# Low halves and sums of the feed-forward part shared between VectorE and GpSimd, and inputs laid out by the host, in a hybrid decoder layer

## The chip, the cores and the metric

One core of one Trainium2 chip runs the whole layer. The metric is the device time of one execution in microseconds (us). The engines are TensorE (PE; its weight loads are PEld in the profile), VectorE (DVE), ScalarE (ACT), GpSimd (POOL) and SyncE (SP), which issues every DMA of this kernel.

## What is computed

The layer takes 2048 tokens of width 1024 in float32. It has a combined projection, a short causal convolution beside dilated attention, an output projection, a feed-forward part with a gated convolution, and a gate on a per-layer input `p`:

```python
h = rmsnorm(x, g_mix[i]);  z = h @ w_in[i]
zb, zc, zx, zq, zk, zv = jnp.split(z, ...)
y_c = zb * causal_dwconv3(zc * zx, conv_w[i], conv_b[i])
y_a = dilated_attention(rmsnorm(zq), rmsnorm(zk), zv)      # three dilations, merged
x = x + concatenate([rmsnorm(y_c, g_out_conv[i]), rmsnorm(y_a, g_out_attn[i])]) @ w_out[i]
h = rmsnorm(x, g_ffn[i])
gate = causal_dwconv3(h @ w_gate[i], ffn_conv_w[i], ffn_conv_b[i])
x = x + (jax.nn.silu(gate) * (h @ w_up[i])) @ w_down[i]    # D_FF = 2816
x = x + sigmoid(rmsnorm(x, g_ple[i]) @ w_ple_gate[i]) * (p[i] @ w_ple_proj[i])
```

## The kernel before

**Precision by halves.** Each operand of a product is split in two. `split` lets ACT copy the float32 value to the reduced type (the high half, L91) and another engine subtract that from the value (the low half, L92). `mm3` (L95) then makes three matmuls: high by high, high by low, low by high. A product on 128x512 tiles is a run of such triples in one PSUM bank.

**Stages.** `qkv` makes q, k and v (until about 347 us of the profile). `mix` runs attention with the convolution's matmuls woven between (until about 995 us). `rest` holds what follows: `project` (the output projection; part 0 of the token groups 0 and 1 first, from 995 us, then part 1, then both parts of groups 2 and 3), `prepare` (normalised tokens as the right-hand operands of the feed-forward part), `gate_up` and `down`, each run for two halves `h` of the tokens, `prepare_ple` and `ple`.

**The feed-forward part** saves matmuls by combining blocks before and after (seven products where eight would stand). `gate_up` runs over `f` = 0 to 10, once per half. For each `f` it makes seven products of gate and seven of up (168 matmuls of 128x512). `left` makes the seven weight operands from raw tiles: four sums on DVE (L706) and seven splits, low halves on POOL. DVE reads the products from PSUM (L757, L991, L1000, L1002), applies the two tap lines of the convolution (L257, L258) and multiplies (L1003); POOL makes four sums of the results (`combined`, L1011). In the first half two side jobs run along: `sums_of_w_down` loads two tiles of `w_down`, makes four differences on POOL (L963) and stores them, for each `f`; `for_later` normalises the other half's tokens on DVE (L792) and stores them. `down` splits one activation tile (low half on DVE) and one weight tile (low half on POOL) for every twelve matmuls, adds earlier sums on POOL (L1052), and meanwhile lets `right` prepare the next stage's operands: differences on DVE (L726), and low halves on the engine that each `put` names.

**What sets the order.** The instructions of an engine run in the order in which a scheduler put them down when the kernel was built. It works from its own estimate of times, so a change in one place can shift the order elsewhere. An engine that waits for one operand holds back all that stands behind it. SP issues DMAs in one such row too.

**Loads of tokens.** The tokens of `x`, `p` and the output are used in an order in which 32 neighbouring rows of a tile lie 16 rows apart in memory. `tokens` (L69) therefore issues four DMAs per tile, one for each group of 32 partitions. `qkv` loads 16 tiles of `x` this way, `project` 32 half tiles, `ple` 16 tiles of `p` and 32 half tiles of output. The convolution's taps `fcw`, `fcb`, `cw`, `cb` and the gains `go`, `gk`, `gq` are read one element at a time.

```python
def split(self, hi, lo, src, lo_engine):
    self.nc.scalar.copy(hi, src)
    lo_engine.tensor_tensor(lo, src, hi.bitcast(F32), ALU.subtract)
```

## Time and profile before

| | us |
|---|---|
| median of 3 runs (2838.21 to 2851.06) | 2841.0 |
| the profiled execution | 2845.52 |
| its span | 2843.8 |
| PE busy in the span | 2638.9 (93%) |
| DVE busy | 1908.9 (67%) |
| POOL busy | 1520.2 (53%) |
| ACT busy | 1320.3 (46%) |

The profile is of one execution. Matmuls are pipelined and their ends are modelled, so the share of a busy PE says less than where PE stood idle and what ended that. The list of waits names, for each engine and line, what it waited for. A timeline gives single instructions with their duration; a table of windows gives busy times in stretches that are named by their start and end in us from the span's start, with the granted clock of PE (1.00 is 2.4 GHz, 0.50 is 1.2 GHz), the DMA engines' busy share and the rate.

### The profile page before, as it was taken

Reading aid. Unit: us, or ns where it says so; the run is one execution under the profiler, and the core shown is the slowest. Engines: PE = TensorE matmul, PEld = TensorE weight load, DVE = VectorE, ACT = ScalarE, POOL = GpSimd, SP = SyncE. Lnnn points to the kernel's source line nnn. Section 1 sums busy time; section 2 is a strip of 40 time slices with the busy share of each in tenths; the row PEclk is TensorE's granted clock in tenths of the full one; section 3 lists DMA queues with packets and bytes.
Section 4 is the critical chain, followed back from the end, with each engine's and each line's share of the span. In section 5 each row is a group of like instructions: output and inputs, shape, how many; then the busy total and the mean of one; then the engine's idle time right before and its main releaser. Section 6 shows DMA issues by size and latency. Waiting matters only on the chain. (4 is left out here: it accounts for less than half of the span.)

```text
span 2843.8 us, 38213 instructions
## 1 busy us (share of the span) xinstructions
PE 2638.9 (93%) x12320; PEld 2174.1 (76%) x12320; DVE 1908.9 (67%) x3355; ACT 1320.3 (46%) x2941; POOL 1520.2 (53%) x1050
## 2 busy tenths in 40 slices
PE   6999989999899869899889999999999999998998
PEld 5777778888788658677677787877878777786787
DVE  8776656767676555987767778457677776647543
ACT  3322257767768234453334444444444445444332
POOL 4111311624343724478786678575666668767554
PEclk9999989999899989999999999999999999999999
DMA  6444566675755778665552236673323326665343
GB/s 185 149 136 124 174 151 152 182 173 148 196 154 152 213 222 306 195 224 205 199 193 97 97 125 213 232 240 106 101 102 104 112 89 212 222 227 195 97 124 88
DMA packets 374473, 470.10 MB, mean 165 GB/s; under 512 B 51072, under 2 KB 214528, under 8 KB 374272
## 3 DMA queue, kind: packets, MB, share of 16 engines
q1 hardware_dynamic: 374272, 467.66, 53.2%
q8 instruction: 97, 1.59, 0.2%
q14 instruction: 104, 0.85, 0.1%
HBM read 339.53 MB, written 127.99 MB: 164 GB/s over the span
## 5 line engine op out<-in xcount | busy, mean ns | idle before, releaser
L95 PE MATMUL ps<-t,w 128*128 128x512 f32 x4368 | 1034.4, 396 | 45.9 <-DVE u L757 23.1
L95 PEld LDWEIGHTS ps<-t,w 128*128 128x128 f32 x4368 | 819.8, 189 | 247.2 <-DVE u L757 28.7
L92 POOL TENSOR_TENSOR w<-raw,w 128x512 fp32r<-128x512 f32 x318 | 477.3, 1510 | 298.4 <-ACT w L91 281.9
L92 POOL TENSOR_TENSOR w<-s,w 128x512 fp32r<-128x512 f32 x208 | 298.8, 1441 | 178.4 <-ACT w L91 172.4
L95 PE MATMUL ps<-w,g 128*128 128x512 f32 x1368 | 342.6, 399 | 52.9 <-ACT g L828 22.3
L95 PEld LDWEIGHTS ps<-w,g 128*128 128x128 f32 x1368 | 258.2, 191 | 118.8 <-ACT g L828 24.9
L290 POOL TENSOR_TENSOR clo<-craw,chi 128x512 fp32r<-128x512 f32 x96 | 125.8, 1317 | 394.7 <-ACT chi L289 132.1
L95 PE MATMUL zps<-hq,chi 128*128 128x512 f32 x768 | 257.1, 412 | 9.2 <-DVE yc L329 5.9
L91 ACT CAST w<-raw 128x512 fp32r<-128x512 f32 x318 | 192.5, 615 | 94.1 <-PE ps L95 90.8
L91 ACT CAST w<-s 128x512 fp32r<-128x512 f32 x208 | 127.9, 617 | 228.3 <-PE ps L95 196.2
L95 PE MATMUL ps<-w,t 128*128 128x512 f32 x852 | 212.1, 395 | 6.8 <-POOL w L92 4.7
L440 ACT ACTIVATE pt<-so,md 128x256 f32<-128x256 f32 (+1 forms) x384 | 174.9, 457 | 84.5 <-DVE md L437 82.6
L95 PEld LDWEIGHTS ps<-w,t 128*128 128x128 f32 x852 | 160.8, 190 | 44.8 <-POOL w L92 7.3
L437 DVE CUSTOM_DVE_ANT_0 so<-s,neg 128x256 f32<-128x256 f32 (+1 forms) x384 | 130.3, 362 | 64.8 <-PE s L434 53.1
L706 DVE TENSOR_TENSOR s<-raw 128x512 f32<-128x512 f32 x88 | 113.4, 1289 | 83.4 <-POOL w L92 82.5
L95 PEld LDWEIGHTS zps<-hq,chi 128*128 128x128 f32 x768 | 142.1, 196 | 35.2 <-DVE yc L329 7.2
L92 DVE TENSOR_TENSOR g<-g 128x512 fp32r<-128x512 f32 x84 | 97.2, 1162 | 98.2 <-ACT g L91 93.2
L95 PE MATMUL zps<-hq,clo 128*128 128x512 f32 x384 | 154.5, 403 | 0.0
L433 PE MATMUL s<-kk,qs 128*128 128x256 f32 (+1 forms) x384 | 132.9, 353 | 20.6 <-DMA kk<-kd 18.2
L434 PE MATMUL s<-kk,qs 128*128 128x256 f32 (+1 forms) x384 | 137.1, 361 | 14.8 <-DMA v<-vd 5.8
L174 POOL TENSOR_TENSOR raw<-hT 128x1024 f32<-128x1024 f32 x16 | 39.0, 2438 | 202.4 <-DVE rs_h L78 187.5
L473 DVE TENSOR_TENSOR nb<-po,nb 64x512 f32<-64x512 f32 x96 | 92.1, 959 | 63.9 <-ACT nb L472 62.9
(214 smaller groups left out, 5118.4 us busy)
## 6 DMA issues: line engine op xcount, KB each, us to landing
gd<-t SPq DMA_DIRECT2D x110, 256.0 KB, 2.0
craw<-in_w_in_dram SPq DMA_DIRECT2D x96, 256.0 KB, 4.0
raw<-in_w_gate_dram SPq DMA_DIRECT2D x44, 512.0 KB, 3.7
raw<-in_w_up_dram SPq DMA_DIRECT2D x44, 512.0 KB, 3.5
g<-gd SPq DMA_DIRECT2D x84, 256.0 KB, 4.3
raw<-td SPq DMA_DIRECT2D x40, 512.0 KB, 4.0
t<-gd SPq DMA_DIRECT2D x70, 256.0 KB, 4.3
v<-vd SPq DMA_DIRECT2D x264, 64.0 KB, 2.6
```

The costliest lines, as they stand in the source:

```text
L91: self.nc.scalar.copy(hi, src)
L92: lo_engine.tensor_tensor(lo, src, hi.bitcast(F32), ALU.subtract)
L95: mm = lambda *a, **k: self.nc.tensor.matmul(*a, **k, **kw)
L174: nc.gpsimd.tensor_tensor(t, hT[:, :, 0].bitcast(F32), hT[:, :, 1].bitcast(F32), ALU.add)
L290: nc.gpsimd.tensor_tensor(lo, raw, hi.bitcast(F32), ALU.subtract)
L433: mm(s[:, lo:], qb[l], cols[0], start=True, stop=False)
L434: mm(s[:, lo:], qb[l], cols[1], start=False, stop=True)
L437: nc.vector.tensor_tensor_reduce(out=so[:, lo:], in0=s[:, lo:], in1=neg[:, br, lo:], scale=-slope, scalar=3.0e38, op0=ALU.add, op1=ALU.min ...
L440: nc.scalar.activation(pt[:, l, lo:], so[:, lo:], AF.Exp, bias=md[:, 0, col:col + 1], scale=-1.0, accum_out=md[:, 1, col:col + 1])
L473: nc.vector.tensor_tensor(dst, like(po[other], br), dst, ALU.add)
L706: nc.vector.tensor_tensor(t, x, y, op)
```

## The change

Three things are changed.

- **Two of three low halves and sums go to VectorE.** A new method `shared` counts calls and returns DVE twice, then POOL once. It now names the engine for the low halves of all weight operands of `project`, `gate_up` and `down`, of the left operands of `ple`, for the sums of squares before `project` and for the sums L1052 in `down`.
- **Fixed moves to VectorE.** The four differences of `sums_of_w_down` go to DVE, as do two of the four sums in `combined` (the other two stay on POOL), two of the four fixed `put`s in `right`, and all low halves that `prepare_ple` names by its own engine.
- **Layout by the host.** `lay_out` permutes `x`, `p` and the weights before the launch, and the output is permuted back after it. `tokens` becomes one DMA per tile. The weight tiles of `w_in`, `w_gate` and `w_up` and the small vectors are contiguous for each partition.

```diff
     def tokens(self, tile, dram, c, j, store=False):
-        for b in range(4):
-            rows, part = dram[c, 4 * j + b], tile[32 * b:32 * b + 32]
-            self.nc.sync.dma_start(*((rows, part) if store else (part, rows)))
+        self.nc.sync.dma_start(*((dram[c, j], tile) if store else (tile, dram[c, j])))
...
+    def shared(self):
+        self.turn = (self.turn + 1) % 3
+        return self.nc.vector if self.turn else self.nc.gpsimd
...
-                nc.sync.dma_start(gk[64 * i:64 * i + 64], a["k_norm_g"].rearrange("(d o) -> d o", o=1))
...
+                nc.sync.dma_start(gk, a["k_norm_g"])
...
-                    nc.sync.dma_start(raw, wv[:, k:k + 2, c0:c0 + 512])
+                    nc.sync.dma_start(raw, a["w_qkv"][w, :, k:k + 2])
...
-            nc.sync.dma_start(raw, self.a["w_in"].rearrange("(k p) n -> p k n", p=P)[:, k:k + 4, c0:c0 + P])
+            nc.sync.dma_start(raw, self.a["w_conv"][z, :, k:k + 4])
...
-                        yield w.rearrange("(k p) n -> p k n", p=P)[:, :, 2 * f * P:2 * f * P + 2 * P]
+                        yield w[f]
...
-                        self.split(t[:, 0], t[:, 1], raw[0][:, i], nc.gpsimd)
+                        self.split(t[:, 0], t[:, 1], raw[0][:, i], self.shared())
...
-            for i in range(3):
-                nc.sync.dma_start(cw[:, :, i], a["ffn_conv_w"][i].rearrange("(k p) -> p k", p=P))
-            nc.sync.dma_start(cb, a["ffn_conv_b"].rearrange("(k p) -> p k", p=P))
+            nc.sync.dma_start(cw, a["ffn_conv_w"])
+            nc.sync.dma_start(cb, a["ffn_conv_b"])
...
-                    self.split(view(t[:, 0]), view(t[:, 1]), x, nc.gpsimd)
+                    self.split(view(t[:, 0]), view(t[:, 1]), x, self.shared())
...
-                put(4, t1, nc.gpsimd)
+                put(4, t1, nc.vector)
...
-                put(6, t3, nc.gpsimd)
+                put(6, t3, nc.vector)
...
-                    nc.gpsimd.tensor_tensor(ssq, ssq, y, ALU.add)
+                    self.shared().tensor_tensor(ssq, ssq, y, ALU.add)
...
-                minus = lambda t, x, y: nc.gpsimd.tensor_tensor(t, x, y, ALU.subtract)
+                minus = lambda t, x, y: nc.vector.tensor_tensor(t, x, y, ALU.subtract)
...
-                        nc.gpsimd.tensor_tensor(t, x, y, op)
+                        (nc.gpsimd if m in (3, 6) else nc.vector).tensor_tensor(t, x, y, op)
...
-                            nc.gpsimd.tensor_tensor(x, x, addend[j], ALU.add)
+                            self.shared().tensor_tensor(x, x, addend[j], ALU.add)
...
-                                     [b[0], b[3], b[1], b[2]], nc.gpsimd)
+                                     [b[0], b[3], b[1], b[2]], nc.vector)
...
+def lay_out(a):
+    by = lambda t, shape, *axes: np.ascontiguousarray(t.reshape(shape).transpose(axes))
+    tokens = lambda t: by(t, (NQ, 32, 16, -1), 0, 2, 1, 3).reshape(SEQ, -1)
...
+        w_gate=by(a["w_gate"], (KD, P, NF // 2, 2 * P), 2, 1, 0, 3), w_up=by(a["w_up"], (KD, P, NF // 2, 2 * P), 2, 1, 0, 3),
```

The lines behind each changed place shift by a few numbers: L69 becomes L66, L92 becomes L94, L706 becomes L702, L757 becomes L753, L963 becomes L959.

SP in the first part of `project`. The names are: `t` rows of x to be added to, `e` and `s` rows of the attention's and the convolution's results (`yad`, `ycd`), `xd` the stored sums. Before:

```order
L823 DMA e<-yad_85 128x512
L823 DMA e<-yad_86 128x512
L823 DMA e<-yad_87 128x512
L823 DMA e<-yad_88 128x512
L69 DMA t<-in_x_dram 32x512 x2
L908 DMA xd_93<-t 128x512
L908 DMA xd_94<-t 128x512
L69 DMA t<-in_x_dram 32x512
L908 DMA xd_95<-t 128x512
L908 DMA xd_96<-t 128x512
L69 DMA t<-in_x_dram 32x512 x13
L823 DMA s<-ycd_81 128x512
```

And with the change:

```order
L328 DMA ycd_84<-yc 128x512
L66 DMA t<-in_x_dram 128x512 x8
L819 DMA e<-yad_85 128x512
L819 DMA e<-yad_86 128x512
L819 DMA e<-yad_87 128x512
L819 DMA e<-yad_88 128x512
L819 DMA s<-ycd_81 128x512
L819 DMA s<-ycd_82 128x512
L819 DMA s<-ycd_83 128x512
```

The loads `s<-ycd` stood behind a long run of issues for x and behind the stores `xd` of token group 1; they now follow eight whole loads of x and four of `e`, ahead of any store.

DVE in `gate_up` of the first half, within one `f` (f = 2): `u`, `e` and `t` are results from PSUM and rows made of them, `s` sums of raw weight tiles, `w` weight operands, `g` tiles of `w_down`. Before:

```order
L757 TENSOR_TENSOR u_14076<-ps_13996,u_14015 128x512
L991 TENSOR_TENSOR e_14097<-ps_13997,u_14076 128x512
L251 MEMSET e_14118 128x2
L706 TENSOR_TENSOR s_14284<-raw_14078,raw_14079 128x512
L991 TENSOR_TENSOR e_14118<-ps_13996,u_14015 128x512
L706 TENSOR_TENSOR s_14286<-s_14284,raw_14078 128x512
L257 SCALAR_TENSOR_TENSOR t_14120<-e_14118,fcw_11136,t_14120 128x512
L991 TENSOR_TENSOR e_14151<-ps_13997,u_14032 128x512
```

And with the change:

```order
L753 TENSOR_TENSOR u_13925<-ps_13845,u_13864 128x512
L257 SCALAR_TENSOR_TENSOR t_13900<-e_13898,fcw_11083,t_13900 128x512
L987 TENSOR_TENSOR e_13946<-ps_13846,u_13925 128x512
L250 MEMSET e_13967 128x2
L959 TENSOR_TENSOR g_15378<-g_15379,g_15378 128x512
L702 TENSOR_TENSOR s_14133<-raw_13927,raw_13928 128x512
L94 TENSOR_TENSOR w_13985<-raw_13774,w_13985 128x512
L959 TENSOR_TENSOR g_15379<-g_15379,g_15378 128x512
L959 TENSOR_TENSOR g_15379<-g_15379 128x512
L987 TENSOR_TENSOR e_13967<-ps_13845,u_13864 128x512
L94 TENSOR_TENSOR w_14041<-s_14039,w_14041 128x512
L702 TENSOR_TENSOR s_14135<-s_14133,raw_13927 128x512
```

Low halves (L94) and differences of `w_down` (L959) now stand between the reads from PSUM.

POOL in `down` of the first half, where every low half of a weight tile stood:

```order
L92 TENSOR_TENSOR w_17726<-raw_17683,w_17726 128x512
L92 TENSOR_TENSOR w_17759<-raw_17683,w_17759 128x512
L92 TENSOR_TENSOR w_17781<-raw_17724,w_17781 128x512
L92 TENSOR_TENSOR w_17803<-raw_17724,w_17803 128x512
L92 TENSOR_TENSOR w_17825<-raw_17779,w_17825 128x512
L92 TENSOR_TENSOR w_17844<-raw_17779,w_17844 128x512
```

And with the change:

```order
L94 TENSOR_TENSOR w_17381<-raw_17316,w_17381 128x512
L94 TENSOR_TENSOR w_17444<-raw_17379,w_17444 128x512
L94 TENSOR_TENSOR w_17510<-raw_17467,w_17510 128x512
L94 TENSOR_TENSOR w_17575<-raw_17532,w_17575 128x512
L94 TENSOR_TENSOR w_17652<-raw_17573,w_17652 128x512
```

Of two tiles of one raw load both stood on POOL; now every third tile of the stream does, and the others stand on DVE.

## Rows read from the trace of the kernel before

**Rows 1.** The page, busy time, share of the span and instructions of each engine.

```profile
PE 2638.9 (93%) x12320; PEld 2174.1 (76%) x12320; DVE 1908.9 (67%) x3355; ACT 1320.3 (46%) x2941; POOL 1520.2 (53%) x1050
```

**Rows 2.** Waits of PE, 0 to 50 us: us in total, times, longest.

```profile
PE ps L95 <- DVE hT L125: 4.7, 1, 4.7
PE tp L122 <- DVE rs_h L78: 4.0, 1, 4.0
```

**Rows 3.** Waits of PE, 995 to 1066 us (first part of `project`).

```profile
PE ps L95 <- ACT g L828: 22.3, 3, 18.2
```

**Rows 4.** Waits of PE, 1235 to 1470 us (`gate_up`, first half, f 0 to 4).

```profile
PE ps L95 <- DVE u L757: 17.7, 11, 4.1
PE ps L95 <- ACT w L91: 5.8, 2, 5.1
PE ps L95 <- POOL w L92: 3.8, 4, 1.4
```

**Rows 5.** Waits of PE, 1450 to 2660 us.

```profile
PE ps L95 <- POOL w L92: 31.9, 31, 3.8
PE ps L95 <- DVE u L757: 6.2, 4, 2.5
```

**Rows 6.** Windows: us, PE, PEld, DVE, ACT, POOL busy (instructions), PEclk, DMA share, GB/s.

```profile
995.00:1000.00 5.00, 3.20 (x14) 2.31 (x14) 3.58 (x6) 1.38 (x3) 0.00 (x0) 1.00 0.89 6
...
995.00:1066.00 71.00, 46.76 (x198) 36.84 (x198) 36.06 (x66) 25.79 (x42) 19.46 (x14) 0.86 0.77 220
1066.00:1140.00 74.00, 74.00 (x339) 60.76 (x338) 41.79 (x90) 31.43 (x66) 30.95 (x23) 1.00 0.85 301
...
1140.00:1235.00 95.00, 84.47 (x381) 66.78 (x380) 85.31 (x135) 51.52 (x101) 43.31 (x30) 0.96 0.60 198
...
1272.50:1466.10 193.60, 169.97 (x724) 134.06 (x723) 137.10 (x137) 74.59 (x159) 158.67 (x107) 0.96 0.60 209
1466.10:1700.50 234.40, 231.02 (x996) 186.38 (x995) 171.79 (x192) 98.37 (x211) 154.64 (x107) 1.00 0.33 110
```

**Rows 7.** Timeline of DVE, 1356 to 1362 us: start, duration, instruction.

```profile
1356.76 1.77 DVE L706 TENSOR_TENSOR s<-raw 128x512 f32<-128x512 f32 x1
...
1361.79 0.68 DVE L757 TENSOR_TENSOR u<-ps,u 128x512 f32<-128x512 f32 x1
```

**Rows 8.** Timeline of POOL, the same stretch.

```profile
1356.24 1.73 POOL L92 TENSOR_TENSOR w<-raw,w 128x512 fp32r<-128x512 f32 x1
```

**Rows 9.** Single lines, whole run: duration in ns, min/median/max, first and last start.

```profile
L706 DVE TENSOR_TENSOR s<-raw x88: 675/1760/1787, 1208.8 to 2341.9; 128x512 f32<-128x512 f32 x88
...
L757 DVE TENSOR_TENSOR u<-ps,u x104: 673/678/694, 1244.9 to 2826.0; 128x512 f32<-128x512 f32 x104
...
L258 DVE SCALAR_TENSOR_TENSOR t<-e,fcw,t x88: 735/1549/1783, 1251.2 to 2365.4; 128x512 f32<-128x512 f32 x88
...
L92 POOL TENSOR_TENSOR w<-raw,w x318: 1267/1304/2348, 937.8 to 2599.9; 128x512 fp32r<-128x512 f32 x159
```

**Rows 10.** Groups by line, 1272.5 to 1466.1 us: busy, mean ns, idle before.

```profile
L706 DVE TENSOR_TENSOR s<-raw 128x512 f32<-128x512 f32 x16 | 25.1, 1567 | 22.8 <-POOL w L92 22.8
...
L963 POOL TENSOR_TENSOR g<-g 128x512 f32<-128x512 f32 x34 | 50.1, 1475 | 24.7 <-DMA g<-in_w_down_dram 19.2 <-issue 2.7 <-DVE u L1002 2.4
```

**Rows 11.** Timeline of SP, 992 to 1037 us: start, time to issue, DMAs.

```profile
992.67 3.94 SPq L682 DMA_DIRECT2D fcw<-in_ffn_conv_w_dram  x3
...
1003.55 11.34 SPq L69 DMA_DIRECT2D t<-in_x_dram  x18
...
1030.08 5.90 SPq L69 DMA_DIRECT2D t<-in_x_dram  x13
1036.08 0.37 SPq L823 DMA_DIRECT2D s<-ycd  x1
```

**Rows 12.** Timeline of SP at the start.

```profile
4.53 2.27 SPq L69 DMA_DIRECT2D xt<-in_x_dram  x4
```

**Rows 13.** Timeline at the end, last stores of the output.

```profile
2836.87 4.50 SPq L69 DMA_DIRECT2D out_dram<-s  x8
```

More of the change, by code (lines that the diff above doesn't have):

```diff
@@ L45, in __init__ @@
         nc = self.nc
+        self.turn = 0
         self.const = ctx.enter_context(tc.tile_pool(reuse_waits="tile", name="const", bufs=1))
@@ L60, in __init__ @@
         self.td = [d.tile([NF // 2, P, 2, 512], F32, name=f"td{i}") for i in range(2)]
-        self.xq = a["x"].rearrange("(c a b) m -> c b a m", a=32, b=16)
-        self.pq = a["p"].rearrange("(c a b) m -> c b a m", a=32, b=16)
-        self.oq = out.rearrange("(c a b) m -> c b a m", a=32, b=16)
+        self.xq, self.pq, self.oq = [t.rearrange("(c j r) m -> c j r m", c=NQ, r=P) for t in (a["x"], a["p"], out)]
     def tokens(self, tile, dram, c, j, store=False):
-        for b in range(4):
-            rows, part = dram[c, 4 * j + b], tile[32 * b:32 * b + 32]
-            self.nc.sync.dma_start(*((rows, part) if store else (part, rows)))
+        self.nc.sync.dma_start(*((dram[c, j], tile) if store else (tile, dram[c, j])))
     def rsqrt(self, pool, ss, n, scale):
@@ L145, in gains @@
             def gains():
-                for i in range(2):
-                    nc.sync.dma_start(gk[64 * i:64 * i + 64], a["k_norm_g"].rearrange("(d o) -> d o", o=1))
-                    nc.sync.dma_start(gq0[64 * i:64 * i + 64], a["q_norm_g"].rearrange("(d o) -> d o", o=1))
+                nc.sync.dma_start(gk, a["k_norm_g"])
+                nc.sync.dma_start(gq0, a["q_norm_g"])
                 for p in range(4):
@@ L154, in qkv @@
             whl = {w: [(wvp if w == 2 else wp).tile([P, KD, 512], F32R, name=f"w{w}{s}") for s in "hl"] for w in range(3)}
-            wv = a["w_in"].rearrange("(k p) n -> p k n", p=P)
             def load_w(w):
@@ L159, in load_w @@
                     raw = stage.tile([P, 2, 512], F32, name="raw", tag="raw")
-                    c0 = 3 * CW + 512 * w
-                    nc.sync.dma_start(raw, wv[:, k:k + 2, c0:c0 + 512])
+                    nc.sync.dma_start(raw, a["w_qkv"][w, :, k:k + 2])
                     self.split(whl[w][0][:, k:k + 2], whl[w][1][:, k:k + 2], raw, nc.gpsimd if w or k % 4 else nc.vector)
@@ L281, in load_conv_w @@
         nc, pool = self.nc, self.cwp
-        c0 = CW * (1, 2, 0)[n % 3] + P * (n // 3 % 4)
+        z = 4 * (1, 2, 0)[n % 3] + n // 3 % 4
         halves = []
@@ L300, in conv @@
         cb = cp.tile([P, 4], F32, name="cb")
-        for i in range(3):
-            nc.sync.dma_start(cw[:, :, i], a["conv_w"][i].rearrange("(k p) -> p k", p=P))
-        nc.sync.dma_start(cb, a["conv_b"].rearrange("(k p) -> p k", p=P))
+        nc.sync.dma_start(cw, a["conv_w"])
+        nc.sync.dma_start(cb, a["conv_b"])
         carry = cp.tile([P, 4, 2, 2, 1], F32, name="carry")
@@ L676, in rest @@
             go = cp.tile([P, 2, 4], F32, name="go")
-            for i, n in enumerate(("g_out_conv", "g_out_attn")):
-                nc.sync.dma_start(go[:, i], a[n].rearrange("(k p) -> p k", p=P))
+            nc.sync.dma_start(go, a["g_out"])
             cw = cp.tile([P, NF, 3], F32, name="fcw")
             cb = cp.tile([P, NF], F32, name="fcb")
-            for i in range(3):
-                nc.sync.dma_start(cw[:, :, i], a["ffn_conv_w"][i].rearrange("(k p) -> p k", p=P))
-            nc.sync.dma_start(cb, a["ffn_conv_b"].rearrange("(k p) -> p k", p=P))
+            nc.sync.dma_start(cw, a["ffn_conv_w"])
+            nc.sync.dma_start(cb, a["ffn_conv_b"])
             carry = cp.tile([P, NF, 2, 1], F32, name="fcarry")
@@ L1183, in steps @@
     return r
+def lay_out(a):
+    by = lambda t, shape, *axes: np.ascontiguousarray(t.reshape(shape).transpose(axes))
+    tokens = lambda t: by(t, (NQ, 32, 16, -1), 0, 2, 1, 3).reshape(SEQ, -1)
+    w_in, g_out = a.pop("w_in"), np.stack([a.pop("g_out_conv"), a.pop("g_out_attn")])
+    return dict(
+        a, x=tokens(a["x"]), p=tokens(a["p"]), g_out=by(g_out, (2, 4, P), 2, 0, 1),
+        w_conv=by(w_in[:, :3 * CW], (KD, P, 12, P), 2, 1, 0, 3), w_qkv=by(w_in[:, 3 * CW:], (KD, P, 3, 512), 2, 1, 0, 3),
+        conv_w=by(a["conv_w"], (3, 4, P), 2, 1, 0), conv_b=by(a["conv_b"], (4, P), 1, 0),
+        q_norm_g=np.tile(a["q_norm_g"], 2)[:, None], k_norm_g=np.tile(a["k_norm_g"], 2)[:, None],
+        w_gate=by(a["w_gate"], (KD, P, NF // 2, 2 * P), 2, 1, 0, 3), w_up=by(a["w_up"], (KD, P, NF // 2, 2 * P), 2, 1, 0, 3),
+        ffn_conv_w=by(a["ffn_conv_w"], (3, NF, P), 2, 1, 0), ffn_conv_b=by(a["ffn_conv_b"], (NF, P), 1, 0))
 def build(shapes):
@@ L1203 @@
     arrays = {n: np.ascontiguousarray(v[0]) for n, v in arrays.items()}
+    arrays = lay_out(arrays)
     arrays["steps"] = steps()
@@ L1206 @@
     r = run_bass_kernel_spmd(nc, [{f"in_{n}_dram": v for n, v in arrays.items()}], core_ids=[0])
-    return r.results[0]["out_0_dram"].reshape(1, SEQ, D)
+    return np.asarray(r.results[0]["out_0_dram"]).reshape(NQ, 16, 32, D).transpose(0, 2, 1, 3).reshape(1, SEQ, D)
```

## The prediction

> **What bounds the kernel now.** I read the busy line first [rows 1]: PE is busy 93% of the span of 2843.8 us, DVE 67%, POOL 53%. PE executes the same matmuls after the change, so what can be won is the time in which PE stands idle, 2843.8 − 2638.9 = 205 us. Busy shares can't tell which of it this change reaches; the waits of PE by stage can, so I read those next. In the stages that the change touches they are: 8.7 us at the start [rows 2], 22.3 in the first part of `project`, one of them 18.2 long [rows 3], 27.3 in f0 to f4 of `gate_up` [rows 4], and 31.9 on low halves from POOL in all that follows, 31 waits of about 1 us [rows 5]. `mix` keeps its order of matmuls and its engines; I give it nothing. The windows [rows 6] say what a stage takes when nothing is late: six `f` of the first half take 234.4 us with PE busy for 231.0, so 39.1 us each; the four before them take 193.6, so 37 are lost there.
>
> Timelines of DVE and POOL in that stretch show why DVE's `u` comes late there. L706, a sum of two tiles in SBUF, takes 1.77 us while a low half runs on POOL beside it [rows 7, 8]; L757, which reads PSUM, takes 0.68 next to it. Over the whole run L706 takes 0.675 at least and 1.76 at the median, L757 never more than 0.69, and POOL's low half 1.30 at the median and 2.35 at most [rows 9]. So a POOL instruction that meets a two-input one of DVE costs DVE up to 1.76 − 0.68 = 1.08 us. Taking POOL instructions away therefore shortens DVE's other work, and this is what pays for most of the work that DVE gets.
>
> **The change part by part.** *The start.* A whole tile of x is one issue and not four of 2.27 us together [rows 12], and the gains come in fewer DMAs. PE's two waits there end on the norm of these tokens [rows 2]. I take 4 of 8.7; ends 0 and +8.
>
> *First part of `project`.* SP needs 3.94 us for three loads of taps, 11.34 for 18 quarter tiles of x and 5.90 for 13 more; only at 1036.08 does it come to `s<-ycd`, on which L828 waits, and PE with it [rows 11, 3]. By the new order eight whole loads of x stand there and `s<-ycd` ahead of any store. 31 issues in 17.2 us are 0.56 each, so 24 quarters fewer are 13 us of issuing. At the stretch's beginning the DMA engines are 0.89 busy at 6 GB/s [rows 6], with the taps read element by element; that also goes. How much can be won? The stage moves 220 GB/s × 71 us = 15.6 MB, which at the 301 GB/s of the next stretch [rows 6] takes 52 us; so 19 at most. I take 16; ends 8 and 20. The transfers may be the next thing that is late.
>
> *`prepare` of the first half and `project` of groups 2 and 3* (1140 to 1235 us): DVE is already busy for 85.3 of 95 us [rows 6]. It gets about two thirds of the low halves of this stretch, some 20 × 0.68 = 13 us. Against that stand up to 20 meetings with POOL less, at 1.08 each. I take 0; ends −6 and +6.
>
> *`gate_up`, f1 to f4 of the first half.* DVE and POOL run in lockstep here: DVE's L706 waits 22.8 us for POOL's low halves, and POOL, with 158.7 of 193.6 us busy, waits another 19.2 at L963 for `w_down` [rows 6, 10]. In f1 to f3 the new order gives DVE 174 instructions where it had 102: 36 differences L959, 28 low halves, 6 sums and 2 others. At their shortest durations [rows 9] (33 reads of PSUM at 0.68, 26 of the tap lines at 0.74, the rest at 0.68) that is about 120 us against 70, or 40 per `f`. POOL keeps 14/3 = 4.67 low halves and 2 sums per `f`, which cost DVE 6.67 × 1.08 = 7.2 us if each meets one of its instructions. So DVE needs 47 us per `f`, and becomes the bound for three `f`; the fourth may run at 39.1. 3 × 47 + 39.1 = 180 against 193.6: a gain of 13.5. But POOL's waits for `w_down` in these three `f`, some 19.2 × 3/4 = 14, may now be DVE's, with the reads of PSUM behind them: then 194. PE is late by whichever DVE does last. I take +4; ends −10 (both the waits and half of the former loss) and +14. If nothing met on the two engines, the term would be 193.6 − 4 × 40 = +34; that is the first rival.
> The Trainium skill ("SBUF — State Buffer", section "SBUF: two separate sides") states that the pair of ports which VectorE and GpSimd share is an exclusive lock held for a whole instruction, and that the loser blocks fully. In that form a meeting costs DVE the whole POOL instruction, which the row has at 1.30 us and not 1.08: over the 20 POOL instructions of f1 to f3 that is 4.4 us more and would take this term to about 0, the forecast to about 2803. The durations of L706 (1.76 at the median, 1.79 at most, against 0.68 alone) bear out the blocking but put its price at 1.08.
>
> *Low halves after 1450 us.* 31.9 us of waits have POOL's low half as their last releaser [rows 5]: in-order POOL at 1.3 us per tile, with sums and stores of other stages between. Two thirds of the low halves leave POOL, so 21 us of these waits go with them. The third that stays finds a less crowded POOL: I let half of 10.6 go, +5. DVE's own new waits (low halves behind reads of PSUM, or the other way round: `u` waits were 6.2 here [rows 5]) I put at −8, somewhat more than these 6.2. Sum +18; ends +5 and +28.
>
> *Steady `gate_up`* (the rest of the first half, the second half; 17 `f`): DVE has 192 instructions in six `f`, 171.8 us busy [rows 6]; 32 per `f`, 21.3 us at their shortest, the other 7.3 us being stretch. It gets 9.33 low halves and 2 sums: 29.0. With 6.67 POOL instructions at 1.08 it is 36.2 of 39.1 us. So it fits with 7% to spare: 0, and this is the tightest place of the whole sum. The other end is 1 to 1.2 us for each of the 17 where in-order waits use up the spare, −20; +5 at best, since PE's 3.4 idle us in six `f` leave no more.
>
> *The end.* The last stores take 4.50 us of issuing for eight [rows 13]; two whole ones instead: +1.5, ends 0 and +3.
>
> Sum: 4 + 16 + 0 + 4 + 18 + 0 + 1.5 = 43.5 us. Against the profiled execution, 2845.5 (span and 1.7 around it), this is 2802. That execution lies 4.5 us above the median of the runs, 2841.0, so the forecast is 2841.0 − 43.5 = 2797.5.
>
> **The rivals.** *Better: the two engines no longer meet.* If POOL's few instructions fall into DVE's idle times or beside reads of PSUM, DVE needs 40 us per `f` in f1 to f3, all of rows 4 and nearly all of rows 5 goes, and the terms become 8, 19, 6, 34, 28, 5, 3: 103 at the very most. A half of the step from 43.5 to there gives 2768, and I let this case span 2740 to 2770. For it: POOL is busy for less than half of what it was. Against: today's median of L706 is the stretched one [rows 9], and six or seven POOL instructions per `f` stay. Chance 0.18.
>
> *Slower: DVE takes POOL's place as the bound.* DVE is in-order, and each low half must wait for ACT's high half, with reads of PSUM queued behind it, for which PE's banks wait. With 36.2 of 39.1 us used, it decides when DVE loses over 7% of its time to such waits. At 15% an `f` takes 36.2/0.85 = 42.6, which is 3.5 more, times 17: −60; f1 to f3 take 47/0.85 = 55 each, so that term is 193.6 − 204 = −10; of the low-half waits 5 are left as gain, and start, `project` and end keep their 21.5. Net −44: 2885; at 12%, 41.1 and 53.4 each, the terms are −35, −6, +5 and +21.5, so −14 and 2855. For it: 30 to 37 of DVE's instructions per `f` then stand in one row with the PSUM reads. Against: at 1140 to 1235 us DVE is busy for 90% [rows 6] with PE still busy for 89%. Chance 0.10, with 2850 to 2885.
> The exclusive lock of the Trainium skill's page "SBUF — State Buffer" (same section) would speak for this rival, since with 1.30 a meeting DVE's 36.2 would be 37.7 of 39.1.
>
> *The loads of `project` are hidden behind another limit.* If not SP's issuing but the transfers or the stores of `yad` and `ycd` end last, the wait [rows 3] shrinks by 5 and not 16. For it: the DMA engines are 0.77 busy in this stretch. Against: `s<-ycd` itself is only issued at 1036 [rows 11]. 2797.5 + 11 = 2808.5; together with the lower half of the low-half term it reaches 2815 to 2835. Chance of this case 0.17: two thirds of it end near 2820 to 2835, within 0.5% of before or close to it.
>
> *That the change does not do what it says* I can exclude: in its instruction order the low halves stand on DVE, and the loads of x are whole.
>
> **How the numbers follow.** Forecast 0.55, within 2778 to 2815. Better 0.18, the loads and small gains 0.17, slower 0.10. The range leaves out the far half of the better case and the slower case: 2756 to 2838. About 0.5% of 2841, 14 us, is what a measurement of this kernel can tell from no change: faster means below 2827, slower above 2855. Faster: the forecast, the better case and a third to a half of the third, 0.77; same 0.15; slower 0.08, the part of the slower case above 2855.
>
> **What would show each step.** In the profile after: SP's issues of x whole, `s<-ycd` issued before about 1025 us, and the 18.2 us wait on L828 gone; if it only moves to a DMA, the third case holds. DVE's L702 with a median below the 1.76 of L706. DVE busy at 2000 to 2100 us, POOL at 700 to 800. In f1 to f4 a spacing near 47 us, in the others 39 to 39.5; 41 or more there is the slower case, 40 or 41 in f1 to f3 the better one. PE's waits on POOL's low halves after 1450 us down to 5 to 10 us; waits on DVE's `u` or DVE's low halves above 15 us would say that DVE took over what POOL gave up. What would make the prediction wrong most easily is this last point: work moved to the engine that drains PSUM.

## The result, and the profile after

| | us | ratio to before, 95% interval |
|---|---|---|
| before, median of 4 | 2842.9 | |
| changed, median of 4 (2758.95 to 2762.15) | 2760.3 | 0.9707 [0.9683, 0.9731] |
| changed, profiled execution | 2758.95 | |

The change takes 82.5 us off the median, nearly twice the 43.5 that the forecast names; the time lies in its range, near the low end. The two profiled executions differ by 86.6. The table puts that difference to stages: it compares when PE starts the n-th of its 12320 matmuls in each profile, counted in time order. (A few matmuls change places in the feed-forward part, so a border there is good to a microsecond or so. From the last start to the end of the span it is 7.0 us before and 6.3 after, which the table leaves out.) The last two columns are for two experiments described below, the layout alone (E1) and the moves alone (E2).

| matmuls | stage | before | changed | gain | E1 | E2 |
|---|---|---|---|---|---|---|
| first start | | 10.9 | 9.0 | 1.9 | 8.7 | 11.2 |
| 0 to 1400 | `qkv` | 322.8 | 320.3 | 2.5 | 319.1 | 320.9 |
| 1400 to 4800 | `mix`, mainly | 666.2 | 651.4 | 14.8 | 655.9 | 658.9 |
| 4800 to 5000 | `project`, first part | 69.7 | 51.8 | 17.9 | 50.2 | 67.9 |
| 5000 to 5900 | `project`, `prepare`, f0 and f1's start | 216.1 | 207.4 | 8.7 | 215.6 | 210.6 |
| 5900 to 6600 | `gate_up` f1 to f4, mainly | 188.0 | 172.1 | 15.9 | 186.8 | 169.7 |
| 6600 to 7650 | f5 to f10 | 246.9 | 242.1 | 4.8 | 246.7 | 242.1 |
| 7650 to 9000 | `prepare`, `down` | 329.9 | 326.1 | 3.8 | 330.8 | 326.4 |
| 9000 to 10300 | `gate_up`, second half | 308.2 | 300.3 | 7.9 | 308.2 | 300.3 |
| 10300 to the last start | `down`, `ple` | 477.9 | 470.4 | 7.5 | 476.5 | 470.4 |

The busy line of the page after, to be held against [rows 1]: DVE has 523 instructions more and only 98 us more to do, POOL half of its instructions and half of its time. PE's busy time is 17.4 us less for the same 12320 matmuls, with a mean granted clock of 0.983 where it was 0.977. So a fifth of the 86.6 us does not come out of idle time, as far as the modelled ends of matmuls tell.

```profile
PE 2621.5 (95%) x12320; PEld 2169.0 (79%) x12320; DVE 2006.8 (73%) x3878; ACT 1321.2 (48%) x2941; POOL 784.3 (28%) x527
```

**First part of `project`.** SP's issues, as in [rows 11], and PE's waits from 975 to 1035 us, as in [rows 3]. The taps are one issue, and x comes in whole tiles. Four loads `s<-ycd` go out ahead of x, at 975, as they did before; the one that [rows 11] have at 1036.08, behind the loads of x, is now issued at 987.67. That is 7 us after PE starts the stage, and it was 36. The wait on ACT's `g` is 1.1 us where it was 22.3, and the stage moves 310 GB/s (window below; columns as in [rows 6]).

```profile
972.17 0.44 SPq L678 DMA_DIRECT2D fcw<-in_ffn_conv_w_dram  x1
...
975.22 2.31 SPq L819 DMA_DIRECT2D s<-ycd  x4
...
979.81 3.84 SPq L66 DMA_DIRECT2D t<-in_x_dram  x8
...
987.67 2.44 SPq L819 DMA_DIRECT2D s<-ycd  x3
```

```profile
980.70:1033.00 52.30, 46.91 (x203) 37.53 (x202) 37.17 (x73) 26.26 (x43) 8.69 (x6) 0.97 0.93 310
```

```profile
PE ps L97 <- DVE t L902: 3.2, 1, 3.2
PE ps L97 <- DVE yc L327: 3.1, 1, 3.1
PE ps L97 <- ACT g L824: 1.1, 1, 1.1
```

**f1 to f4 of the first half.** The windows are the single `f`, cut where PE starts each one's first product; columns as in [rows 6]. After the change f1, f2 and f3 take 46.5, 44.9 and 45.9 us, f4 38.9 and the ones behind it 193.9 / 5 = 38.8. In f1 to f3 DVE is busy for 124.3 of 137.3 us, POOL for 36.5.

```profile
1234.00:1280.50 46.50, 43.01 (x200) 34.56 (x198) 42.69 (x59) 21.05 (x44) 15.17 (x7) 1.00 0.82 280
1280.50:1325.40 44.90, 41.90 (x189) 33.36 (x188) 39.20 (x57) 18.50 (x40) 11.92 (x7) 1.00 0.85 279
1325.40:1371.30 45.90, 41.86 (x169) 33.53 (x168) 42.45 (x62) 17.45 (x37) 9.40 (x6) 0.93 0.74 262
1371.30:1410.20 38.90, 38.90 (x170) 31.58 (x170) 30.45 (x44) 16.76 (x36) 10.78 (x7) 1.00 0.31 108
1410.20:1604.10 193.90, 193.90 (x841) 157.75 (x840) 154.81 (x220) 83.30 (x176) 51.09 (x33) 1.00 0.31 104
```

Cut in the same way, four later `f` of the kernel before give 159.2 / 4 = 39.8 each:

```profile
1511.40:1670.60 159.20, 156.23 (x673) 125.90 (x672) 118.19 (x130) 65.88 (x141) 103.95 (x72) 1.00 0.30 101
```

PE's waits from 1180 to 1415 us (against [rows 4]) and from 1400 to 2570 us (the cut of [rows 5]), and DVE's own waits in f1 to f3:

```profile
PE ps L97 <- DVE w L94: 9.0, 5, 4.0
PE ps L97 <- POOL w L94: 2.2, 1, 2.2
PE ps L97 <- DVE u L753: 1.9, 3, 0.6
```

```profile
PE ps L97 <- DVE w L94: 9.2, 9, 1.7
PE ps L97 <- DVE g L94: 5.2, 2, 3.4
...
PE ps L97 <- POOL w L94: 3.5, 6, 0.9
```

```profile
DVE g L959 <- DMA g<-in_w_down_dram: 7.9, 8, 2.0
DVE g L788 <- DMA g<-xd: 3.8, 4, 1.6
```

DVE's reads of PSUM are hardly waited for any more; what PE waits for are DVE's low halves, and 13.1 of the 27.3 us of [rows 4] are left. In f1 to f3 DVE's row is full: 124.3 us of work and 11.7 of waits for loads make 136.0 of the 137.3. L702, which is the stretched L706 of [rows 7, 9], has a median of 0.69 us:

```profile
L702 DVE TENSOR_TENSOR s<-raw x88: 674/691/694, 1161.2 to 2263.7; 128x512 f32<-128x512 f32 x88
```

### The profile page after: what moved, and what is told of

Same layout as the page of the kernel before. It is cut to its first block, busy times and chain, and to the rows that moved or that the text cites. A ratio compares the mean times of both kernels' runs of the same rounds, so it can differ in the third digit from the quotient of the medians.

```text
span 2757.2 us, 37506 instructions
## 1 busy us (share of the span) xinstructions
PE 2621.5 (95%) x12320; PEld 2169.0 (79%) x12320; DVE 2006.8 (73%) x3878; ACT 1321.2 (48%) x2941; POOL 784.3 (28%) x527
## 5 line engine op out<-in xcount | busy, mean ns | idle before, releaser
L94 POOL TENSOR_TENSOR w<-raw,w 128x512 fp32r<-128x512 f32 x100 | 144.9, 1449 | 564.1 <-ACT w L93 364.0
L94 POOL TENSOR_TENSOR w<-s,w 128x512 fp32r<-128x512 f32 x70 | 111.8, 1597 | 368.7 <-ACT w L93 300.0
L97 PEld LDWEIGHTS ps<-w,t 128*128 128x128 f32 x852 | 159.0, 188 | 49.5 <-DVE w L94 8.8
L94 DVE TENSOR_TENSOR w<-raw,w 128x512 fp32r<-128x512 f32 x218 | 177.1, 816 | 15.5 <-ACT w L93 15.5
L431 PE MATMUL s<-kk,qs 128*128 128x256 f32 (+1 forms) x384 | 132.8, 352 | 14.7 <-DMA kk<-kd 12.2
L94 DVE TENSOR_TENSOR g<-g 128x512 fp32r<-128x512 f32 x84 | 72.6, 867 | 88.5 <-ACT g L93 88.5
L453 DVE TENSOR_TENSOR plo<-ptp,phi 128x512 fp32r<-128x512 f32 (+1 forms) x160 | 103.6, 653 | 30.9 <-ACT phi L452 30.2
```

Source lines behind the costliest of these rows:

```text
L97: mm = lambda *a, **k: self.nc.tensor.matmul(*a, **k, **kw)
L431: mm(s[:, lo:], qb[l], cols[0], start=True, stop=False)
L453: nc.vector.tensor_tensor(lo[:, i:i + n], tp[:, :n], hi[:, i:i + n].bitcast(F32), ALU.subtract)
```

## The experiments

What is to be explained: which parts of the change carry the 82.5 us, and why f1 to f4 gave 16 where 4 was forecast. My theory after the result: the layout wins what lies ahead of the feed-forward part, and the moves win the rest because POOL's row no longer holds DVE up. Rivals: the larger pieces of the weights' loads win some of it; `mix` gained by the moves; the low halves, the sums or the differences alone do it. "Changed" below is the changed kernel at 2760.3 us. Each time is set against runs of the kernel before on the same chip; a difference between two variants of under some 6 us is within the intervals.

### E1 and E2: the layout alone, the moves alone

E1 is the changed kernel with each engine name as it was, in these lines and the seven others that the change's diff moves:

```diff
-                        self.split(t[:, 0], t[:, 1], raw[0][:, i], self.shared())
+                        self.split(t[:, 0], t[:, 1], raw[0][:, i], nc.gpsimd)
...
-                minus = lambda t, x, y: nc.vector.tensor_tensor(t, x, y, ALU.subtract)
+                minus = lambda t, x, y: nc.gpsimd.tensor_tensor(t, x, y, ALU.subtract)
```

E2 is the kernel before with those nine lines as the change has them, and none of its layout:

```diff
-                        self.split(t[:, 0], t[:, 1], raw[0][:, i], nc.gpsimd)
+                        self.split(t[:, 0], t[:, 1], raw[0][:, i], self.shared())
...
-                minus = lambda t, x, y: nc.gpsimd.tensor_tensor(t, x, y, ALU.subtract)
+                minus = lambda t, x, y: nc.vector.tensor_tensor(t, x, y, ALU.subtract)
```

> The host's layout and whole DMAs alone; every low half, sum and difference stays on the engine that had it before. The two profiles place 82 us of gain: 4 at the start, 15 in mix, 18 in the first part of project, 7 in project and prepare up to 1262 us, 18 in gate_up f0 to f4, and some 25 after that. Theory A, the layout carries what lies before 1140 us and nothing else: 4 + 15 + 18 = 37, plus 1.5 at the end, so 2800 to 2808. Theory B (the prediction's split), mix has no part in it and its 15 us come with the moved engines or with a shifted order: 21.5, so 2818 to 2824. Theory C, fewer and larger DMA packets also feed gate_up better: 2770 to 2790, and PE's loss in f1 to f4 falls with it.

> The moves to VectorE alone, with the layout and the DMAs of before. Theory A: 7 + 18 + 25 less the 1.5 of the end = 45 to 50, so 2793 to 2800, and the 18 us wait on L828 in project is still there. Theory B: 60 to 65, 2778 to 2785. Theory C: under 35, above 2808. If the parts don't add up to 82, one of them needs the other.

E1: 2806.9, ratio 0.9872 [0.9849, 0.9894], 36.6 us less than before. E2: 2790.4, ratio 0.9813 [0.9790, 0.9837], 53.0 less. Together 89.6, against 82.5: they add up within their intervals. The table's last columns show a clean cut: `project`'s first part belongs to the layout, everything from f0 on to the moves. The long wait is still there with the moves alone (PE's waits, 985 to 1060 us of E2):

```profile
PE ps L101 <- ACT g L834: 19.3, 3, 16.1
```

Theory A holds for both, though E2 lies 2.6 us below its range; theories B and C fall. `mix` is less clean: 655.9 with the layout, 666.2 before, but also 658.9 with the moves alone, which change nothing there.

### E3 and E4: the small pieces of the weights' loads

```diff
-            nc.sync.dma_start(raw, self.a["w_conv"][z, :, k:k + 4])
+            nc.sync.dma_start(raw, self.a["w_cin"].rearrange("(k p) n -> p k n", p=P)[:, k:k + 4, c0:c0 + P])
```

```diff
-                        yield w[f]
+                        yield w.rearrange("(k p) n -> p k n", p=P)[:, :, 2 * f * P:2 * f * P + 2 * P]
```

> The changed kernel with only the convolution's weights (craw) read as before, in pieces of 512 bytes. Theory A, these small pieces crowded the DMA engines in mix and made kk, v and the rest of attention's loads late: mix loses its 15 us again, 2772 to 2777. Rival, mix gained by a shifted order of instructions or by one execution's chance: within 4 us of the changed kernel, 2757 to 2764.

> The changed kernel with only w_gate and w_up read as before, in pieces of 1 KB. In the steady part of gate_up an f took 38.8 us after against 39.6 before (200 matmuls in 46.2 and 47.2 us). Theory A, that 0.8 us per f is won on the engines: no change, 2757 to 2764. Theory C, it is won by the larger pieces: 14 to 17 f lose 0.8 each and f0 to f4 lose more, 2773 to 2785.

E3: 2764.6, ratio 0.9722 [0.9692, 0.9752]; E4: 2756.7, ratio 0.9693 [0.9669, 0.9717]. Neither can be told from the changed kernel. The `f` of the second half are as short with pieces of 1 KB (300.3 us in both profiles), so the layout of `w_gate` and `w_up` brings nothing. For the convolution's weights the medians differ by 4.3 us, and the interval reaches to 13 above the changed kernel. So most of theory A's 12 to 17 us is excluded, and no gain is shown.

### E5: four DMAs per tile of tokens

```diff
-        self.nc.sync.dma_start(*((dram[c, j], tile) if store else (tile, dram[c, j])))
+        for b in range(4):
+            rows, part = dram[c, j][32 * b:32 * b + 32], tile[32 * b:32 * b + 32]
+            self.nc.sync.dma_start(*((rows, part) if store else (part, rows)))
```

> The changed kernel with each tile of tokens moved in four DMAs of 32 rows again (neighbouring rows now); all else as changed. The first part of project took 69.7 us before and 51.8 after (PE's matmuls 4800 to 5000). Theory A, SP's issuing set that part: it goes back to 65 or more, start and end lose 2 to 4, together 2776 to 2784. Rival, the taps read element by element held the DMA engines there, and issuing was hidden: the part stays below 55, 2760 to 2766.

2774.6, ratio 0.9757 [0.9737, 0.9778]: 14 us given back, 1.4 us short of theory A's range. `project`'s first part takes 65.6 us again, 13.8 of its gain of 17.9. The start gives back all that it had won (PE's first start at 11.2 us, then 323.0 for `qkv`), while f1 to f4 win 4.7 in a different order. SP's row and PE's wait (975 to 1060 us) are those of before, with the same bytes and contiguous rows:

```profile
986.21 10.69 SPq L68 DMA_DIRECT2D t<-in_x_dram  x21
...
1020.19 0.40 SPq L821 DMA_DIRECT2D s<-ycd  x1
```

```profile
PE ps L99 <- ACT g L826: 18.3, 3, 14.8
```

So it is the number of issues in SP's row, at 0.51 us each here: from the first of these lines to the second it issues 48 quarter tiles in 24.3 us, where the changed kernel issues 8 whole tiles in 3.84. The other 4 us of that stage may be those of the taps, which E5 still reads whole; that part was not tried alone.

### E6: the differences of `w_down` back on POOL

```diff
-                minus = lambda t, x, y: nc.vector.tensor_tensor(t, x, y, ALU.subtract)
+                minus = lambda t, x, y: nc.gpsimd.tensor_tensor(t, x, y, ALU.subtract)
```

> The changed kernel with the four differences of sums_of_w_down back on GpSimd, all else as changed. After the change an f takes 46.5, 44.9 and 46.0 us in f1 to f3, with VectorE busy for 46.3, 43.0 and 46.0 of them, and 38.8 in the rest. Theory A, VectorE's work is the bound there: it loses 12 differences per f, f1 to f3 fall to 40 to 42, 2745 to 2752. Rival, it was GpSimd's row of low halves and differences with its waits for w_down that held PE before, and this alone brings it back: f1 to f3 at 48 or more, 2766 to 2775.

2772.9, ratio 0.9752 [0.9733, 0.9771]: 12.5 us slower than the changed kernel, the time that the rival names, with POOL at half of its time; its 48 us or more for f1 to f3 did not come. By the starts of their first products f0 to f4 take 51.2, 46.5, 47.2, 46.0 and 42.8 us, 12.8 more than changed (44.7, 46.5, 44.9, 46.0, 38.8): 6.5 of it in f0, 4.0 in f4 and 2.3 in f1 to f3. The waits of POOL and of DVE in f1 to f3 show one way in which POOL's row costs time:

```profile
POOL g L959 <- DMA g<-in_w_down_dram: 44.4, 11, 9.1
```

```profile
DVE s L702 <- POOL w L94: 11.5, 5, 3.2
```

POOL stands 44.4 of 139.6 us at differences whose tiles have not come, with low halves behind them, and DVE stands behind those. On DVE the same differences waited 7.9 us. But in f0, where half of the loss lies, DVE never waits for POOL. It is busy for longer there with fewer instructions (windows of f0, E6 and then the changed kernel):

```profile
1196.00:1247.20 51.20, 43.23 (x185) 34.10 (x184) 46.82 (x62) 22.94 (x51) 29.08 (x19) 0.97 0.66 228
```

```profile
1189.30:1234.00 44.70, 41.33 (x186) 32.88 (x184) 41.37 (x70) 21.70 (x49) 10.55 (x7) 1.00 0.65 223
```

Over the shortest duration of each kind in the run DVE's instructions last 15.4 us longer in E6's f0, with 19 POOL instructions beside them, and 5.2 longer in the other, with 7. So an idle POOL is no free place: what counts is what is queued behind its waits, and what its instructions meet on DVE.

### E7 and E8: the whole share on DVE, and one third of it

```diff
-        return self.nc.vector if self.turn else self.nc.gpsimd
+        return self.nc.vector
```

```diff
-        return self.nc.vector if self.turn else self.nc.gpsimd
+        return self.nc.gpsimd if self.turn else self.nc.vector
```

> The changed kernel with the whole share on VectorE: no low half of a weight and no sum of the share stays on GpSimd. In a steady f VectorE is busy for 33.5 of 38.8 us; it gets 4.67 low halves of 0.68 = 3.2 and loses about as much stretch. Theory A, the work fits: steady f at 38.8 still, f1 to f3 within 2 us of before, 2755 to 2768. Theory B (the prediction's slower rival), at some load VectorE's row of low halves and reads of PSUM makes PE late: steady f above 39.5, 2785 or more.

> The changed kernel with the share turned round: one of three on VectorE, two on GpSimd. In a steady f GpSimd has 9.3 low halves and 2 sums, some 17 us, against 17 to 19 instructions and 26.5 us before. If the waits on GpSimd's low halves grow with its load, a steady f takes 39.2 to 39.5 and the time is 2768 to 2780. If the 0.9 us wait per f came from one fixed place in the row, which the share only moves, f is either 38.8 or 39.8 and the time 2760 or 2785. VectorE's sum L702 should be stretched again, its median near 1 us or above.

E7: 2748.4, ratio 0.9667 [0.9647, 0.9687]; E8: 2761.2, ratio 0.9706 [0.9681, 0.9730]. With all of it DVE is not the bound in a steady `f` (38.8 us still), and f1 to f3 take 47.6, 43.3 and 41.5, 5 us less than changed; the time is 7 us below the range that I gave it. So the slower rival of the prediction has no ground even with more work on DVE. In f1 to f3 the rows of E7 also divide DVE's time (window, then DVE's waits):

```profile
1234.30:1366.70 132.40, 125.69 (x553) 100.15 (x552) 118.66 (x189) 57.06 (x122) 9.85 (x6) 0.99 0.82 283
```

```profile
DVE g L959 <- DMA g<-in_w_down_dram: 8.2, 8, 1.8
DVE g L788 <- DMA g<-xd: 5.5, 3, 3.4
```

118.7 us of work and 13.7 of waits for loads make the whole 132.4. With POOL down to 6 instructions DVE works 39.6 us per `f`, next to the 40 that the prediction has for that case; what lies above it is waiting.

With one third on DVE the time is that of two thirds: so in a steady `f` the waits do not grow with POOL's share, as one of my two expectations had it. The time fits the other, by which they come from one fixed place in the row. Four steady `f` of E8 take 155.2 / 4 = 38.8 us, with POOL at 69.6 and DVE at 117.8:

```profile
1448.60:1603.80 155.20, 155.20 (x673) 126.23 (x672) 117.83 (x155) 66.24 (x141) 69.58 (x46) 1.00 0.31 104
```

My expectation that L702 would be stretched again was wrong: its median there is 0.691, and only its maximum is back at 1.78. Over the runs the stretch goes with the time for which these sums wait for POOL: of 88 sums 49 last over 1.5 us in the kernel before, with 82.5 us of such waits, 38 in E10 (67.1), 11 in E8 (23.9) and none in the changed kernel (10.9). That a sum which POOL releases starts together with POOL's next instruction would fit this, but was not tested.

```profile
L702 DVE TENSOR_TENSOR s<-raw x88: 676/691/1780, 1162.9 to 2261.5; 128x512 f32<-128x512 f32 x88
```

### E9: the differences spread over all `f`

The change's share is on DVE whole, as in E7, and each step of `sums_of_w_down` waits for a row of its own `f`.

```diff
-            def sums_of_w_down(f):
+            def sums_of_w_down(f, after):

                 b = [operand("g").bitcast(F32) for _ in range(2)]
+                for t in b:
+                    nc.scalar.copy(t[:, 0, :1], after[:, :1])
...
-                        sums_of_w_down(f)
+                        sums_of_w_down(f, ts[1, 0])
```

> The whole share on VectorE, as in the run with all of it there, and the load of each step of sums_of_w_down made to wait for a row of its own f: ScalarE copies one element per partition of that row into the tile before the load overwrites it. So four differences stand in each f and no longer all 44 in f0 to f3, where VectorE was busy for 44 to 47 us per f and f took 46.0, 47.6, 43.3 and 41.5. Theory A, VectorE's amount of work is what bounds f0 to f3: with 7 to 9 differences fewer per f they fall by 4 to 6 us each, the later f stay at 38.8 (34.4 of work plus 2.7), and the time is 2728 to 2738 against 2748. Rival, it is the chain from ScalarE's high halves or the normalised tokens of the other half that sets them: within 4 us of 2748.

2734.9, ratio 0.9611 [0.9587, 0.9635]: 13.5 us under E7, 25 under the changed kernel, and the fastest version here. PE has no wait at all from 1190 to 1360 us. f1 to f3:

```profile
1235.10:1275.60 40.50, 40.50 (x186) 33.22 (x185) 36.80 (x58) 18.88 (x41) 3.36 (x2) 1.00 0.57 205
1275.60:1315.20 39.60, 39.60 (x177) 32.35 (x176) 33.57 (x52) 17.65 (x39) 3.29 (x2) 1.00 0.39 136
1315.20:1354.90 39.70, 39.70 (x178) 32.39 (x176) 34.76 (x56) 18.03 (x39) 2.98 (x2) 1.00 0.59 211
```

They are 0.8 us and more above 38.8 because eight transposes for the other half's tokens, sixteen in f1, run in them. So DVE's row is what bounds f1 to f3 of E7 and of the changed kernel. This run does not divide that between DVE's work and its waits for loads, since both fell: its waits on `w_down` go from 7.9 to 1.5 us in these three `f`. The rows of E7 do.

### E10 to E12: each kind of move alone, on top of the layout

E10 is E1 with only the first of these lines changed, E11 with only the second, E12 with all the other moves (the share and the fixed low halves) and neither of the two:

```diff
-                minus = lambda t, x, y: nc.gpsimd.tensor_tensor(t, x, y, ALU.subtract)
+                minus = lambda t, x, y: nc.vector.tensor_tensor(t, x, y, ALU.subtract)
...
-                        nc.gpsimd.tensor_tensor(t, x, y, op)
+                        (nc.gpsimd if m in (3, 6) else nc.vector).tensor_tensor(t, x, y, op)
```

> The host's layout with one move alone, the four differences of sums_of_w_down on VectorE; the layout with no move was 2806.8. Putting them back on GpSimd cost the changed kernel 12.5 us. Theory A, their place in GpSimd's row, with the waits for w_down, held up the low halves behind them and is most of what f0 to f4 lost: f1 to f3 from 44 to 49 us down to 43 to 46, steady f still at 39.8, 2788 to 2797. Rival, they matter only once GpSimd is otherwise empty (it still has 18 instructions per f): 2800 to 2808.

> The host's layout with one move alone, two of the four sums L1007 of each f on VectorE. GpSimd's row has its four sums and six low halves without a pause at the end of each f, and PE's one wait per steady f, 0.9 us, follows on a low half some 12 us earlier in the row. Theory A, that crowded end is where the lateness comes from: a steady f falls from 39.8 to 38.8 and 17 f give 14 to 17 us, 2788 to 2794. Rival, the place of the wait has its own cause (ScalarE's high half, then VectorE's stretched sum): f stays at 39.8, 2802 to 2808.

> The host's layout with the shared and fixed low halves on VectorE and neither the differences of w_down nor the sums L1007 moved. Theory A, the low halves are what made a steady f 39.8: it falls to 38.8, f0 to f4 stay slow as in the run with the differences back on GpSimd, 2774 to 2784. If moving the sums alone also gives 38.8, either edit does it and the gains of the parts do not add. Rival, with four sums at its end GpSimd's third of the low halves is still late: f at 39.3 to 39.8, 2790 to 2800.

| on top of the layout (2806.9) | us | ratio to before, 95% interval | f1 to f4 | a steady f |
|---|---|---|---|---|
| E10, differences | 2793.6 | 0.9817 [0.9796, 0.9838] | 43.1, 45.3, 43.5, 48.2 | 39.8 |
| E11, two sums | 2806.7 | 0.9865 [0.9842, 0.9888] | 45.9, 49.5, 49.0, 50.6 | 39.0 to 39.2 |
| E12, low halves | 2785.1 | 0.9789 [0.9768, 0.9811] | 46.4, 46.2, 44.6, 46.5 | 38.8, three of the second half 40.0 |
| all (the change) | 2760.3 | 0.9707 [0.9683, 0.9731] | 46.5, 44.9, 46.0, 38.8 | 38.8 |

The differences are worth 13.3 us, all of it in f0 to f4; the low halves 21.7, with most `f` at 38.8; the sums nothing in the total. Theory A holds for E10, and for E12 but for 1 us above its range. For E11 neither held whole: the wait per steady `f` shrinks from 0.9 to 0.2 to 0.4, yet the total stays. By the stage borders of the table E11 gains 5.5 us in the second half's `gate_up` (302.7) and loses 3.3 in `mix` and 4.9 from 5400 to 6600 against E1, the first of which it does not touch; whether the move costs f0 to f4 anything stays open. The three add up to 35, the whole to 46.5; by the ratios, each to the kernel before on its own chip, it is 41 of 47. So 6 to 11 us may be won only together, which is hardly more than the intervals allow. They do not lie in f1 to f4, where the three give 15.8 (5900 to 6600 of the table) and the whole 14.7. The profiles have 5.9 of them between 5000 and 5900, 7.9 in `prepare` and `down` (330.3 to 333.1 in E10 to E12 against 326.1), and 6.4 in `mix`, which no move touches; what causes them stays open.

Whether f4 is short goes with where the scheduler put the 44 differences of `w_down`. The changed kernel has all of them in f0 to f3, as have E3, E4 and E7, and f4 takes 38.8 or 38.9 in each. E10 has 15 of them in f4 (48.2 us, DVE busy for 45.1 of it and never waiting for POOL), E11 has 11 (50.6), E12 8 (46.5), E2 and E5 11 each (43.8 and 43.7), E8 3 (40.4) and E6 2 (42.8).

## Why the prediction was right in sign and short in size

**Start**, 4 forecast: 4.4 measured (first start and `qkv`). Held in size, and E5 gives it back whole. But 1.9 of it is PE's first start, and of the two waits of [rows 2] that the term names, 8.7 us, 7.8 are left (5.0 and 2.8).

**First part of `project`**, 16: 17.9. Held, with its mechanism (E5: 13.8 of it is SP's issuing), and under the cap of 19: the stage takes 51.8 us at 310 GB/s, where the cap was worked out from 52 us at 301. The 31 issues of the prediction were not all. Between the lines of [rows 11] stand 17 more quarter tiles, so 48 in 25.2 us held up that `s<-ycd`, not 31 in 17.2.

**`project` and `prepare`** (5000 to 5900), 0, ends −6 and +6: 8.7. The term missed. With the moves alone the stretch falls by 5.6, with the layout alone by 0.5. By the modelled ends 5.5 of the 8.7 is PE's busy time, which the prediction took for fixed. It reaches into f0 (47.2 before, 44.7 after), for which the sum had no term of its own: it began at f1.

**f1 to f4**, +4: 15.9. The mechanism was right: DVE's row is the bound for three `f`, and the fourth runs free. The step that failed is the size of DVE's work in it. "So DVE needs 47 us per `f`" stands next to the measured 46.5, 44.9 and 46.0 by luck, for these are not work alone: DVE is busy for 41.4 us per `f` and waits 3.9 for loads. The fear for which I took 4 and not the worked-out 13.5, that POOL's waits for `w_down` would be DVE's "with the reads of PSUM behind them", came true: 7.9 us of them, and 3.8 more for `xd`, against the 14 feared. Work and waits do add up, as in the prediction's 194 (141, 14 and 39.1). They only came to less: 124.3, 11.7, 1.3 of other idle time and 38.9 for f4, together 176. The 47 was too high in two ways. Durations overlap: a DVE instruction of 0.68 us is followed by the next after 0.60 (a timeline of DVE in f1, start and duration first; beside it POOL's):

```profile
1251.15 1.75 DVE L959 TENSOR_TENSOR g<-g 128x512 f32<-128x512 f32 x1
1252.82 1.77 DVE L94 TENSOR_TENSOR w<-s,w 128x512 fp32r<-128x512 f32 x1
1254.52 0.74 DVE L257 SCALAR_TENSOR_TENSOR t<-e,fcw,t 128x512 f32<-128x512 f32 x1
1255.18 0.68 DVE L702 TENSOR_TENSOR s<-raw 128x512 f32<-128x512 f32 x1
1255.79 0.68 DVE L753 TENSOR_TENSOR u<-ps,u 128x512 f32<-128x512 f32 x1
1256.39 0.67 DVE L94 TENSOR_TENSOR w<-raw,w 128x512 fp32r<-128x512 f32 x1
```

```profile
1250.64 1.71 POOL L94 TENSOR_TENSOR w<-raw,w 128x512 fp32r<-128x512 f32 x1
1252.31 1.74 POOL L1007 TENSOR_TENSOR t<-t,c 128x512 f32<-128x512 f32 x1
```

The durations of f1 to f3 sum to 135 us, DVE's busy time there is 124. And not every POOL instruction meets one of DVE's with two inputs from SBUF: over each line's own shortest duration DVE's instructions are stretched by 16 us in these `f`, which have 20 POOL instructions, so 0.8 each and not 1.08. Where they meet, the rows bear out the price: 1.75 and 1.77 beside POOL, 0.68 without. POOL's low half is longer there, too: 1.71, where 1.30 was the median [rows 9]. (The L757 of [rows 7] has no POOL instruction beside it; that reads of PSUM are not stretched rests on the 0.694 us in [rows 9].) The Trainium skill ("SBUF — State Buffer", section "SBUF: two separate sides") states an exclusive lock, from which the prediction worked out 1.30 for each meeting. The trace agrees that the two engines hold each other up, not with that price as a mean; and the forecast by it is 2797.5 + 4.4 = 2802, not 2803.

**Low halves after 1450 us**, +18: the waits on POOL's low halves fell from 31.9 to 3.5, the 6.2 on `u` went as well, and those on DVE's low halves (`w` and `g` after, `g` and `t` before) are 14.4 where they were 3.2: 23.4 net. The stages from 6600 to the last start gained 24.0. Held, though the 14.4 is close to the 15 that the prediction names as the sign that DVE took over what POOL gave up.

**Steady `f`**, 0 with 7% to spare: no loss, and the spare was 20% (154.8 of 193.9 us busy), for the two reasons just named. One of my numbers was wrong underneath: "39.1 us each" for an `f` in which nothing is late. The window held 996 matmuls and not six times 168; an `f` took 39.8, with one wait of 0.9 on POOL in it, and now takes 38.8. I had counted those waits in the term above, so the sum did not suffer, but the base was not free of loss.

**The end**, 1.5: 0.8 from the last start to the end of the span.

**`mix`**, nothing: 14.8 in the profiles. "`mix` keeps its order of matmuls and its engines; I give it nothing" failed. The twelve profiles with the layout have 648 to 659 us there, the two without 666 and 659, so part of it is what one execution differs from the next. By medians E1 gains 36.6, of which its profile finds 5.9 at the start and in `qkv`, 19.5 in `project`'s first part and 2 to 3 later; some 9 are left for `mix`. What of the layout does it (the taps read whole, the convolution's weights, fewer issues) stays open; E3 leaves at most a part to the weights.

**The rivals.** The time is that of the better case, which I gave 0.18, but only half of its mechanism came: L702 no longer meets POOL and the steady `f` have no wait left, while 13.1 of the 27.3 us of [rows 4] stay. f1 to f3 stayed at 45 to 46 us, not at 40; E9 shows that this was still to be had. That the time falls into this case is in part luck: the terms of the sum come to 72 us where 43.5 were forecast, and without the 15 in `mix`, to which no case gave anything, the time would be near 2775, above the case's 2770. Against the slower case stands E7.

## What to carry to other kernels

Two engines that work in one chain and each in order lose more than either one's busy share says: the wait at the head of one row (POOL for a load) becomes the other's wait behind it, so move the instruction that waits first, and look at what is queued behind it where it goes. Price a move by the distance between starts, not by summed durations, and count the instructions of the window from which a base is taken. Size a row's work and its waits as two terms, each against its own row: a wait for a load moves with the instruction that waits (11.7 us here, of 14 forecast). Side work that runs along should be tied to the stage that has room for it: spreading 44 differences over eleven `f` gave 13.5 us that no choice of engine did.
